# An encoder layer on one core: operand buffers of three stages moved, queries transposed without doubled rows, a division moved to VectorE

## The chip, the core and the metric

The kernel runs on one core of a Trainium2 chip. A core has TensorE (matrix products; the profile calls its products PE and its weight loads PEld), VectorE (DVE), ScalarE (ACT), GpSimd (POOL) and SyncE (SP), which here only issues DMAs. Each engine takes its instructions in the order in which they were laid down and stops at one whose operand is not ready. The metric is the device time of one execution in microseconds, the median of several runs. The profile is of one further execution.

## The reference

Two sequences of 512 rows and 1024 columns go through one encoder layer. All of it is float32.

```python
h = rms_norm(x, ln1)
q, k, v, u, g_att, g_ssm = jnp.split(h @ w_in, IN_SPLITS, axis=-1)
q = rms_norm(q.reshape(bsz, seq_len, N_HEADS, HEAD_DIM), q_gain)
k = rms_norm(k.reshape(bsz, seq_len, N_KV_HEADS, HEAD_DIM), k_gain)
y_att = windowed_attention(q, k, v, sink, bias, band_mask(seq_len))
y_ssm = s5_branch(u, ...)        # bidirectional linear recurrence, GELU, gate
mixed = sigmoid(g_att) * y_att + sigmoid(g_ssm) * y_ssm
x = x + mixed @ w_out
h2 = rms_norm(x, ln2)
y = x + jnp.square(jax.nn.relu(h2 @ w_up)) @ w_down
```

The attention has 16 query heads of 64 columns, four to each of 4 key heads. A block of 128 queries sees its own block of keys and its two neighbours, with a relative bias and a sink logit for each head. The MLP is 1024 to 4096 to 1024.

## The kernel before, in words

**Numbers in two parts.** TensorE works on a rounded format (fp32r). To keep float32's precision, every operand is split: `hi` is the value rounded by ScalarE, `lo` the rest, subtracted by VectorE. A product is three matmuls, hi·hi, hi·lo and lo·hi (`mm3`, L148 to L152). Nearly all matmuls have 128 weight columns and a moving operand of 512 (in the projections of queries 256) columns.

**Memory.** SBUF is laid out as two stacks of pools. On the left stand the constants, among them `vec`, a tile of 66 columns (L108), and above it `cpool` (tiles c_hi, c_lo and c_raw, weights split for the column products), `evp` and the pools of each stage. On the right stands first `hT`, the normalised input turned and split, later four slots of 32 KB, `slot_a` to `slot_d`. Sizes of the tiles below a tile fix its address. Worked out from them, before the change the tiles of `cpool`, `evp` and the T4 operand of the up projection start at 352 modulo 512 bytes, and the tiles on the right at 480.

**Stages in order of time** (us of the profile):

- to 233: x is normalised and turned into `hT`, then the tables of the recurrence are built. All through this and the next two stages, column products of `hT` with w_in (L221, a generator called by `pull`) are fed to TensorE as a filler between the stage's own matmuls.
- 233 to 342: the scan, 62 steps of VectorE operations (from L582), each depending on the one before, with filler on TensorE.
- 342 to 481: output of the recurrence, key products (L261), first projections of queries and values.
- 481 to 718: attention, in 8 steps (key head j, sequence sq), numbered 0 to 7.
- 718 to 835: last division of the attention, then the gate (GLU) with products of `act` and c_hi, c_lo.
- 835 to 937: output projection and second norm.
- 937 to 1241: up projection. Sixteen tiles r, for each seven products of one step of a Strassen scheme (a product of 2 by 2 blocks in seven block products; the operands are B11 and B21 in `slot_c`, T1 and B22 in `slot_d`, T2 and T3 in `slot_b`, T4 on the left). The raw weights of the tiles are split into a ring of operands in `slot_a`. Results are rounded through ReLU and square (`relu2`, ScalarE, L1182 and L1183) and stored to `a_scr`.
- 1248 to 1562: down projection, `product_d`, again seven products, each over the 16 tiles taken in pairs.

**The attention's order.** TensorE, ScalarE and VectorE run in the order of the code inside `tc.manual_schedule`; SyncE's and GpSimd's instructions are placed by the planner. Each step has four units (qb 0 to 3, a block of 128 queries each). A unit computes the scores of four heads (`scores`, L764), row maxima (`largest`, VectorE, L768), exponentials (`exp`, ScalarE, L774), and beside them, for the unit before, the transposes of P (`turn`, L780), their split (`high` ScalarE L784, `low` VectorE L789) and the products with V (`value`, L796). `add` (VectorE, L806) joins the two halves of the unit before into `ya`. As fill between them stands `Tile` for the next step: `project` (L711), `square`, `power` (GpSimd, L724), `norm` (VectorE, L728), then the doubling copy on GpSimd (L729), which writes every query's 64 values a second time, so that the transpose (`turn`, L734) gives 128 rows: values in rows 0 to 63 and again in rows 64 to 127. `high` (ScalarE, L739) writes the scaled and rounded values into all 128 rows and `low` (VectorE, L743) then puts the rest into the lower 64, so one matmul of 128 rows multiplies the high and the low part at once with keys that stand in both halves.

**The division.** The softmax is divided at the end. In step i, unit 1, `Divide` takes the row sums of step i−1: `invert` (VectorE), `turn` (a transpose of 16 columns on TensorE, L822, a copy, a DMA of the inverses to `rs_scr`, L825, and two DMAs from there that spread a row over 64 partitions, `fac`, L830). At the end of that unit `multiply` is laid down: GpSimd multiplies `ya` (128 by 1024) by `fac` (L835), and the queue of SyncE stores the result. The last step's division stands alone after the loop, with GpSimd's queue, and the gate's loads of `mx` (L1036) follow it.

**The down projection's buffers.** A pair needs `d_a` (activations from `a_scr`, 4 KB a partition, three buffers), a tile `k1_r` of weights (k1, k2 and k3 stay for later products, 4 KB each), and the split tiles a_hi, a_lo, b_hi, b_lo. Before, the pool `down0` (k1_0 to k1_2, d_a, a_hi) lies in the place of the ring, `down` (a_lo, b_hi, b_lo, xq) in that of `slot_b`, and `downb` (k1_3 to k1_7) in that of `slot_c`. The ring is read until the last product of the last tile, p4; `slot_c` is read last by p2 of that tile.

Of the kernel before, what the change touches and what calls it, by code (L numbers as in the profile page):

```python
# [12 lines left out]
F32 = mybir.dt.float32  # L13
F32R = mybir.dt.float32r
I32 = mybir.dt.int32
AF = mybir.ActivationFunctionType
ALU = mybir.AluOpType
AX = mybir.AxisListType

P = 128  # L20
# [6 lines left out]
HALF = 512  # L27
# [3 lines left out]
G = 4  # L31
HD = 64
# [8 lines left out]
CH = 16  # L41
# [22 lines left out]
def hybrid_layer(ctx, tc, x, rel, onehot, ln1, w_qkv, w_ug, vectors, lam, coefs, w_glu, w_out, ln2,  # L64
                 w_up, w_down, out):
    nc = tc.nc
    V, S, PE, GP, SP = nc.vector, nc.scalar, nc.tensor, nc.gpsimd, nc.sync
    DRAM, PSUM = bass.MemoryType.DRAM, bass.MemoryType.PSUM

    const = ctx.enter_context(tc.tile_pool(name="const", bufs=1))  # L70
# [33 lines left out]
    ident = const.tile([P, P], F32, name="ident")  # L104
    make_identity(nc, ident)
    neg_half = const.tile([P, 16], F32, name="neg_half")
    V.memset(neg_half, -0.5)
    vec_pad = const.tile([P, 66], F32, name="vec")  # L108
    vec = vec_pad[:, 0:58]
    bglu_sb, gain_q, gain_k, nsink = [vec[:, a:b] for a, b in ((0, 8), (8, 9), (9, 10), (10, 26))]  # L110
    dd = vec[:, 26:58].rearrange("p (x g) -> p x g", g=2)
# [58 lines left out]
    cf = coef_cm.__enter__()  # L170
# [9 lines left out]
    fi = cf.tile([P, GROUPS], F32, name="fi")  # L180
    es = cf.tile([P, 9, GROUPS], F32, name="es")
    bs_p = cf.tile([P, GROUPS, T], F32, name="bs_p")
    dmask = cf.tile([P, CH], F32, name="dmask")
    lbt = cf.tile([P, 2, SB, 64], F32, name="lbt")
    columns = [("u", U_BLK + c) for c in range(KT)] + [("a", GA_BLK + c) for c in range(KT)] + [("s", GS_BLK + c) for c in range(KT)]
    loaded, key_tiles, sigmoids = [], [], set()
# [446 lines left out]


    with tc.tile_pool(name="att", bufs=2, reuse_waits="tile") as ap, tc.tile_pool(name="attc", bufs=1, reuse_waits="tile") as ac:
        kn = ac.tile([P, NT, N_KV, HD], F32, name="kn")
        va = ac.tile([P, NT, N_KV, P], F32R, name="va")

# [59 lines left out]
        class Tile:  # L698
# [25 lines left out]
                GP.tensor_tensor(self.rq, ms, neg_half[:, 0:G], op=ALU.pow)  # L724

            def norm(self):
                self.qn = ap.tile([P, G, 2, HD], F32, tag="qn", name="qn")
                V.tensor_mul(self.qn[:, :, 0], self.psv, self.rq[:, :, None].to_broadcast([P, G, HD]))  # L728
                GP.tensor_copy(self.qn[:, :, 1], self.qn[:, :, 0])  # L729

            def turn(self):
                self.pt = acc()
                for h in range(G):
                    PE.transpose(self.pt[:, h * P:(h + 1) * P], self.qn[:, h].rearrange("p a d -> p (a d)"), ident)  # L734

            def high(self):
                self.ptv = self.pt.rearrange("p (h t) -> p h t", h=G)
                self.dst = queries[self.key][:, :, self.t * P:(self.t + 1) * P]
                S.activation(self.dst, self.ptv, AF.Copy, scale=gain_q)  # L739

            def low(self):
                dst = self.dst[64:128]
                V.scalar_tensor_tensor(dst, self.ptv[64:128], gain_q[64:128], dst.bitcast(F32),  # L743
                                       op0=ALU.mult, op1=ALU.subtract)

        class Unit:
# [61 lines left out]
        class Divide:  # L808
# [23 lines left out]

            def multiply(self):
                j, sq = self.j, self.sq
                GP.tensor_tensor(self.ya, self.ya, self.fac, op=ALU.mult)  # L835
                self.queue.dma_start(mix_scr[2 * j:2 * j + 2, :, sq * HALF:(sq + 1) * HALF].rearrange("m p t -> p m t"),
                                     self.ya)

# [52 lines left out]
        with tc.manual_schedule(engines={mybir.EngineType.PE, mybir.EngineType.Activation, mybir.EngineType.DVE}):  # L891
            for i, (j, sq) in enumerate(steps):
                nxt = steps[i + 1] if i + 1 < len(steps) else None
                sums = small.tile([P, G, NB], F32, tag="sm", name="sm", bufs=2)
                ya = ap.tile([P, 2, HALF], F32, tag="ya", name="ya")
                extra = pieces_of(i)
                for qb in range(NB):
                    if 1 <= i < 3:

                        t = (i - 1) * NB + qb  # L900
                        SP.dma_start(y2_scr[:, :, t, :].rearrange("g c k -> c g k"), y_scr[t])
                    cur = Unit(j, sq, qb, sums, ya)
                    n3 = prev.nkb if prev else 0
                    div = Divide(*steps[i - 1], *done) if qb == 1 and i > 0 else None
                    new = Tile(*nxt, qb) if nxt else None
                    project = new.project if new else nop
                    kd = None
                    if rows and not rows.qn:
                        rows.power()
                    cur.scores(0)  # L910
                    cur.largest(0)
                    cur.scores(1)
                    if owed:
                        owed.add()
                    cur.largest(1)
                    if n3:
                        prev.turn(0)
                        prev.high(0)
                    project(6)
                    if n3:  # L920
                        prev.low(0)
                    cur.exp(0)
                    cur.exp(1)
                    if rows and not rows.qn:
                        rows.norm()
                    if qb == 0 and nxt:
                        kd = key_copies(*nxt)
                    if div:
                        div.invert()
                    cur.scores(2)  # L930
                    cur.largest(2)
                    if n3:
                        prev.turn(1)
                        prev.high(1)
                    project(4)
                    if n3:
                        prev.value(0, 0)
                    project(2)
                    cur.exp(2)
                    cur.scores(3)  # L940
                    if lower:
                        lower()
                        lower = None
                    if n3:
                        prev.low(1)
                        prev.value(0, 1)
                    cur.largest(3)
                    if rows:
                        rows.turn()
                    if n3 > 2:  # L950
                        prev.turn(2)
                    if kd:
                        key_turn(*nxt, kd)
                    if div:
                        div.turn()
                    project(4)
                    if rows:
                        rows.high()
                        rows.low()
                    if n3 > 2:  # L960
                        prev.high(2)
                    if n3:
                        prev.value(1, 0)
                    cur.exp(3)
                    if n3 > 2:
                        prev.low(2)
                    project(4)
                    if n3:
                        prev.value(1, 1)
                    project(4)  # L970
                    if n3 > 2:
                        prev.value(2, 0)
                        prev.value(2, 1)
                    if new:
                        new.square()
                    if n3:
                        prev.lower_part()
                    if extra:
                        lower = extra.pop(0)()
                    if div:  # L980
                        div.multiply()
                    owed, prev, rows = prev, cur, new
                    if nxt and qb == NB - 1 and sq == 1:
                        load_biases(nxt[0])
                done = sums, ya
                if i == len(steps) - 2:
                    hpool_cm.__exit__(None, None, None)
                    slot_a = opers.enter_context(tc.tile_pool(name="slot_a", bufs=1, side="right", reuse_waits="tile"))
                    slot_b = opers.enter_context(tc.tile_pool(name="slot_b", bufs=1, side="right", reuse_waits="tile"))
                    yT = [slot(slot_b), slot(slot_a)]  # L990
# [9 lines left out]
        div = Divide(*steps[-1], *done, True)  # L1000
# [231 lines left out]
    opers.close()  # L1232


    with tc.tile_pool(name="down0", bufs=2, side="right", reuse_waits="tile") as d0, \
            tc.tile_pool(name="down", bufs=2, side="right", reuse_waits="tile") as dp, \
            tc.tile_pool(name="downb", bufs=1, side="right", reuse_waits="tile") as db, \
            tc.tile_pool(name="downc", bufs=1, reuse_waits="tile") as dc:

        k1 = [(d0 if r < 3 else db).tile([P, 2, HALF], F32, name=f"k1_{r}", bufs=1) for r in range(NPAIR // 2)]  # L1240
        k2, k3 = [[dc.tile([P, 2, HALF], F32, name=f"k{i}_{r}") for r in range(NPAIR // 2)] for i in (2, 3)]
        q1, q3, q4, q5 = [dc.tile([P, 4, HALF], F32, name=f"q{i}") for i in (1, 3, 4, 5)]

        def product_d(n):

# [149 lines left out]
```

## Time and profile before

| what | value |
|---|---|
| median of 3 runs | 1566.19 us (1565.89 to 1566.23) |
| the profiled execution, time | 1564.48 us |
| its span | 1562.7 us |
| mean granted TensorE clock | 0.986 |
| ScalarE busy | 771.0 us (49%) |
| GpSimd busy | 231.0 us (15%) |
| DMA | 237.07 MB, 152 GB/s on the mean |

The page of the profile gives busy time by engine, the chain of work that ended last, and the costliest groups: `line engine op out<-in partitions x elements xcount | busy, mean ns of one | idle time of the engine before them and what ended it`. `L1263 ACT CAST a_hi<-d_a ... x56 | 59.0, 1054` is line 1263 on ScalarE, 56 times, 59.0 us in all, 1054 ns each. In a timeline, each row is a start, a duration, an engine, a line and an operation, and in brackets how long the engine sat idle before it and what it waited for. A row of the view by windows gives the stretch, its length, busy time and count for TensorE, its weight loads, VectorE, ScalarE and GpSimd, then the granted TensorE clock, the mean busy share of the DMA engines and GB/s. Matmuls overlap in their records, so their rate is read from start to start, not from a duration. PEq, ACTq and SPq are the sequencers of the engines, which issue DMAs.

### The profile page before, as it was taken

Reading aid. Unit: us, or ns where it says so; the run is one execution under the profiler, and the core shown is the slowest. Engines: PE = TensorE matmul, PEld = TensorE weight load, DVE = VectorE, ACT = ScalarE, POOL = GpSimd, SP = SyncE. Lnnn points to the kernel's source line nnn. Section 1 sums busy time; section 2 is a strip of 40 time slices with the busy share of each in tenths; the row PEclk is TensorE's granted clock in tenths of the full one; section 3 lists DMA queues with packets and bytes.
Section 4 is the critical chain, followed back from the end, with each engine's and each line's share of the span. In section 5 each row is a group of like instructions: output and inputs, shape, how many; then the busy total and the mean of one; then the engine's idle time right before and its main releaser. Section 6 shows DMA issues by size and latency. Waiting matters only on the chain.

```text
span 1562.7 us, 21589 instructions
## 1 busy us (share of the span) xinstructions
PE 1480.6 (95%) x7818; PEld 1242.0 (79%) x7818; DVE 1104.4 (71%) x1989; ACT 771.0 (49%) x1349; POOL 231.0 (15%) x412
## 2 busy tenths in 40 slices
PE   5899999999999999988799989999999899999998
PEld 4688888878999888975577867888888687888787
DVE  8688849985436888896875558777777478566553
ACT  6577761224436788785333335544455334433332
POOL 3133332002331333323320000000000000000000
PEclk9899999999999999999899999999999999999999
DMA  5644438227751323125745234444443694455332
GB/s 180 213 156 158 146 137 301 101 88 268 266 169 40 104 56 101 62 77 174 228 148 170 81 108 138 155 155 159 157 153 122 228 340 145 148 161 163 121 122 68
DMA packets 103532, 237.07 MB, mean 152 GB/s; under 512 B 11994, under 2 KB 31706, under 8 KB 103424
## 3 DMA queue, kind: packets, MB, share of 16 engines
q1 hardware_dynamic: 64784, 134.82, 27.0%
q0 software_dynamic: 16464, 50.39, 9.8%
q10 hardware_dynamic: 22176, 50.47, 8.4%
q8 instruction: 62, 1.02, 0.3%
q14 instruction: 46, 0.38, 0.1%
HBM read 165.35 MB, written 81.82 MB: 158 GB/s over the span
## 4 chain that ended last, share of the span: by engine, by line
PE 40%; issue 7%; DMA 2%; DVE 2%; POOL 2%; ACT 1%; POOLq 0%; ACTq 0%; DVEq 0%; SPq 0%
PE bank L151 13%; PE bank L152 13%; PE bank L150 13%; POOL mx L1036 1%; DMA w_raw<-in_w_out_dram 0%; DMA mx<-ga_scr 0%; DMA k<-in_w_down_dram 0%; DMA fac<-rs_scr 0%; DVE rn_xn L1116 0%; DMA f_raw<-in_w_up_dram 0%; ACT rn_xn L1112 0%; PE acc L152 0%; POOL rs L1115 0%; DMA mx<-mix_scr 0%; PE acc L151 0%
## 5 line engine op out<-in xcount | busy, mean ns | idle before, releaser
L221 PE MATMUL acc<-hT,c_hi 128*128 128x512 f32 x768 | 252.5, 404 | 0.7 <-ACT c_hi L211 0.7
L150 PE MATMUL bank<-b_hi,a_hi 128*128 128x512 f32 x448 | 174.0, 391 | 7.2 <-ACT b_hi L1263 7.2
L151 PE MATMUL bank<-b_lo,a_hi 128*128 128x512 f32 x448 | 175.4, 392 | 2.5 <-DVE b_lo L1264 2.5
L152 PE MATMUL bank<-b_hi,a_lo 128*128 128x512 f32 x448 | 174.8, 390 | 0.0
L221 PEld LDWEIGHTS acc<-hT,c_hi 128*128 128x128 f32 x768 | 142.5, 190 | 32.2 <-issue 2.2
L221 PE MATMUL acc<-hT,c_lo 128*128 128x512 f32 x384 | 154.7, 403 | 0.5 <-DVE c_lo L212 0.5
L150 PE MATMUL bank<-act,act 128*128 128x512 f32 x376 | 147.2, 392 | 3.0 <-ACT act L1161 3.0
L1263 ACT CAST a_hi<-d_a 128x1024 fp32r<-128x1024 f32 x56 | 59.0, 1054 | 183.4 <-PE bank L151 181.0
L151 PE MATMUL bank<-act,act 128*128 128x512 f32 x376 | 146.9, 391 | 0.0
L152 PE MATMUL bank<-act,act 128*128 128x512 f32 x376 | 146.4, 390 | 0.0
L1264 DVE TENSOR_TENSOR a_lo<-d_a,a_hi 128x1024 fp32r<-128x1024 f32 x56 | 68.5, 1224 | 107.4 <-ACT a_hi L1263 107.4
L711 PE MATMUL acc<-w_hi,hT 128*128 128x256 f32 x512 | 115.4, 294 | 0.0
L150 PEld LDWEIGHTS bank<-b_hi,a_hi 128*128 128x128 f32 x448 | 84.4, 189 | 25.3 <-ACT b_hi L1263 7.7
L151 PEld LDWEIGHTS bank<-b_lo,a_hi 128*128 128x128 f32 x448 | 84.5, 189 | 21.5 <-DVE b_lo L1264 4.1
L152 PEld LDWEIGHTS bank<-b_hi,a_lo 128*128 128x128 f32 x448 | 84.5, 189 | 17.6
L711 PEld LDWEIGHTS acc<-w_hi,hT 128*128 128x128 f32 x512 | 86.4, 188 | 3.6
L221 PEld LDWEIGHTS acc<-hT,c_lo 128*128 128x128 f32 x384 | 72.9, 190 | 16.3 <-issue 1.0
L150 PEld LDWEIGHTS bank<-act,act 128*128 128x128 f32 x376 | 71.0, 189 | 18.4 <-ACT act L1161 3.4
L151 PEld LDWEIGHTS bank<-act,act 128*128 128x128 f32 x376 | 71.0, 189 | 14.8
L152 PEld LDWEIGHTS bank<-act,act 128*128 128x128 f32 x376 | 70.8, 188 | 14.8
L774 ACT ACTIVATE p<-p,nmx 128x257 f32<-128x257 f32 (+1 forms) x128 | 72.2, 565 | 15.9 <-DVE nmx L768 14.9
L1182 ACT ACTIVATE a<-a 128x512 f32<-128x512 f32 x64 | 40.5, 633 | 73.5 <-DVE a L1176 50.3
(316 smaller groups left out, 3536.7 us busy)
## 6 DMA issues: line engine op xcount, KB each, us to landing
d_a<-a_scr SPq DMA_DIRECT2D x56, 512.0 KB, 3.6
u_raw<-in_w_up_dram SPq DMA_DIRECT2D x32, 512.0 KB, 5.6
a_scr<-t ACTq DMA_DIRECT2D x64, 256.0 KB, 5.0
k<-in_w_down_dram SPq DMA_DIRECT2D x32, 512.0 KB, 5.9
c_raw<-in_w_ug_dram SPq DMA_DIRECT2D x48, 256.0 KB, 3.2
a_scr<-a ACTq DMA_DIRECT2D x48, 256.0 KB, 2.2
ct_scr<-ctab POOLq DMA_DIRECT2D x16, 576.0 KB, 4.4
ctab_in<-ct_scr POOLq DMA_DIRECT2D x16, 576.0 KB, 7.2
```

What stands on the lines that cost most here:

```text
L150: PE.matmul(ps, a[0], b[0], start=first, stop=False)
L151: PE.matmul(ps, a[0], b[1], start=False, stop=False)
L152: PE.matmul(ps, a[1], b[0], start=False, stop=last)
L221: PE.matmul(ps, w[wi][:, k, :], hT[s][hi][:, k, :], start=n == 0, stop=n == 3 * KT - 1)
L711: PE.matmul(self.ps, hT[sq][act][:, k, col:col + P], w[:, k % 4, :], start=i == 0, stop=i == 3 * KT - 1)
L774: S.activation(p, p, AF.Exp, bias=self.nmx[:, h:h + 1], scale=-1.0, accum_out=self.sums[:, h, self.qb:self.qb + 1])
L1036: GP.dma_start(t_, scr[m, :, s * HALF:(s + 1) * HALF])
L1182: S.activation(c, c, AF.Relu)
L1263: S.copy(hi, src)
L1264: V.tensor_sub(lo, src, hi.bitcast(F32))
```

## The change

Four things change.

1. **Addresses.** The tile `vec` grows from 66 to 98 columns (128 bytes), and a mask of 16 columns, before in a pool on the right, moves into it. All that stands above it on the left moves up by 128 bytes, `cpool`, `evp` and T4's operand from 352 to 480 modulo 512. In the attention's pool an unused tile of 40 columns is put first, so that its tiles move by 288 bytes in all.
2. **Queries.** `norm` writes 64 values for a query and the copy on GpSimd is gone. The transpose has 64 weight columns and gives 64 rows; `high` writes rows 0 to 63, and `low` reads them there and writes rows 64 to 127.
3. **Division.** `multiply` is VectorE's and stands in unit 3 of the step, behind the first row maximum, no longer at the end of unit 1. The last one is VectorE's too.
4. **Down projection.** `downb` comes first (in the ring's place), filled up with q5 and an unused tile of 4 KB; `down0` comes third (in the place of `slot_c`); `down` stays in that of `slot_b`.

```diff
-    vec_pad = const.tile([P, 66], F32, name="vec")
+    vec_pad = const.tile([P, 98], F32, name="vec")
...
-    dmask = cf.tile([P, CH], F32, name="dmask")
+    dmask = vec_pad[:, 64:64 + CH]
...
+        ap.tile([P, 40], F32, name="apart", bufs=1)
...
-                self.qn = ap.tile([P, G, 2, HD], F32, tag="qn", name="qn")
-                V.tensor_mul(self.qn[:, :, 0], self.psv, self.rq[:, :, None].to_broadcast([P, G, HD]))
-                GP.tensor_copy(self.qn[:, :, 1], self.qn[:, :, 0])
+                self.qn = ap.tile([P, G, HD], F32, tag="qn", name="qn")
+                V.tensor_mul(self.qn, self.psv, self.rq[:, :, None].to_broadcast([P, G, HD]))
...
-                    PE.transpose(self.pt[:, h * P:(h + 1) * P], self.qn[:, h].rearrange("p a d -> p (a d)"), ident)
+                    PE.transpose(self.pt[0:64, h * P:(h + 1) * P], self.qn[:, h], ident)
...
-                S.activation(self.dst, self.ptv, AF.Copy, scale=gain_q)
+                S.activation(self.dst[0:64], self.ptv, AF.Copy, scale=gain_q[0:64])
...
-                V.scalar_tensor_tensor(dst, self.ptv[64:128], gain_q[64:128], dst.bitcast(F32),
+                V.scalar_tensor_tensor(self.dst[64:128], self.ptv, gain_q[0:64], self.dst[0:64].bitcast(F32),
                                        op0=ALU.mult, op1=ALU.subtract)
...
-                GP.tensor_tensor(self.ya, self.ya, self.fac, op=ALU.mult)
+                V.tensor_mul(self.ya, self.ya, self.fac)
...
                     cur.largest(0)
+                    if qb == 3 and late:
+                        late.multiply()
                     cur.scores(1)
...
-                    if div:
-                        div.multiply()
+                    if qb == 1:
+                        late = div
...
-    with tc.tile_pool(name="down0", bufs=2, side="right", reuse_waits="tile") as d0, \
+    with tc.tile_pool(name="downb", bufs=1, side="right", reuse_waits="tile") as db, \
             tc.tile_pool(name="down", bufs=2, side="right", reuse_waits="tile") as dp, \
-            tc.tile_pool(name="downb", bufs=1, side="right", reuse_waits="tile") as db, \
+            tc.tile_pool(name="down0", bufs=2, side="right", reuse_waits="tile") as d0, \
...
+        q5 = db.tile([P, 4, HALF], F32, name="q5")
+        db.tile([P, HALF * 2], F32, name="apart")
...
-        q1, q3, q4, q5 = [dc.tile([P, 4, HALF], F32, name=f"q{i}") for i in (1, 3, 4, 5)]
+        q1, q3, q4 = [dc.tile([P, 4, HALF], F32, name=f"q{i}") for i in (1, 3, 4)]
```

More of the change, by code (lines that the diff above doesn't have):

```diff
@@ L733, in turn @@
                 for h in range(G):
-                    PE.transpose(self.pt[:, h * P:(h + 1) * P], self.qn[:, h].rearrange("p a d -> p (a d)"), ident)
+                    PE.transpose(self.pt[0:64, h * P:(h + 1) * P], self.qn[:, h], ident)
             def high(self):
-                self.ptv = self.pt.rearrange("p (h t) -> p h t", h=G)
+                self.ptv = self.pt[0:64].rearrange("p (h t) -> p h t", h=G)
                 self.dst = queries[self.key][:, :, self.t * P:(self.t + 1) * P]
-                S.activation(self.dst, self.ptv, AF.Copy, scale=gain_q)
+                S.activation(self.dst[0:64], self.ptv, AF.Copy, scale=gain_q[0:64])
             def low(self):
-                dst = self.dst[64:128]
-                V.scalar_tensor_tensor(dst, self.ptv[64:128], gain_q[64:128], dst.bitcast(F32),
+                V.scalar_tensor_tensor(self.dst[64:128], self.ptv, gain_q[0:64], self.dst[0:64].bitcast(F32),
                                        op0=ALU.mult, op1=ALU.subtract)
```

## The prediction

> **What bounds the kernel now.** I read the page first (engine totals, chain of work, costliest groups), then TensorE's waits, then the places that they name.
>
> ```profile
> span 1562.7 us, 21589 instructions
> PE 1480.6 (95%) x7818; PEld 1242.0 (79%) x7818; DVE 1104.4 (71%) x1989; ACT 771.0 (49%) x1349; POOL 231.0 (15%) x412
> PE 40%; issue 7%; DMA 2%; DVE 2%; POOL 2%; ACT 1%; POOLq 0%; ACTq 0%; DVEq 0%; SPq 0%
> ...
> L221 PE MATMUL acc<-hT,c_hi 128*128 128x512 f32 x768 | 252.5, 404 | 0.7 <-ACT c_hi L211 0.7
> L221 PE MATMUL acc<-hT,c_lo 128*128 128x512 f32 x384 | 154.7, 403 | 0.5 <-DVE c_lo L212 0.5
> ```
>
> TensorE is busy for 95% of the span and leads the chain. So the time moves in three ways only: TensorE waits less, its matmuls follow each other faster, or it is made to wait anew. Its list of waits has the two that the change aims at:
>
> ```profile
> PE bank L150 <- ACT b_hi L1263: 7.2, 1, 7.2
> ...
> PE acc L734 <- POOL qn L729: 6.0, 16, 2.2
> ```
>
> The sum is made against the profiled execution, 1564.48 us with a span of 1562.7; the median of the three runs is 1566.19, 1.7 more. I take the difference that I work out off that median.
>
> **A. From up to down projection.** In the timelines of SyncE, ScalarE and TensorE and the table by windows:
>
> ```profile
> 1227.62 2.42 SPq L1253 DMA_DIRECT2D k<-in_w_down_dram  x5
> 1232.83 0.38 SPq L1274 DMA_DIRECT2D xq<-x_scr  x1
> 1241.06 0.33 SPq L1250 DMA_DIRECT2D d_a<-a_scr  x1
> ...
> 1243.46 0.63 ACT L1183 ACTIVATE a<-a 128x512 f32<-128x512 f32 x1 [0.34 <-ACT a L1182]
> 1245.25 1.04 ACT L1263 CAST a_hi<-d_a 128x1024 fp32r<-128x1024 f32 x1 [1.16 <-DMA d_a<-a_scr]
> 1247.39 1.04 ACT L1263 CAST b_hi<-k 128x1024 fp32r<-128x1024 f32 x1 [1.10 <-DMA k<-in_w_down_dram]
> ...
> 1240.87 0.40 PE L152 MATMUL bank<-t,act 128*128 128x512 f32 x1
> 1248.49 1.22 PE L150 MATMUL bank<-b_hi,a_hi 128*128 128x512 f32 x2 [7.22 <-ACT b_hi L1263]
> ...
> 1248.40:1252.50 4.10, 3.98 (x9) 2.67 (x10) 2.45 (x2) 2.09 (x3) 0.00 (x0) 0.50 1.04 415
> ```
>
> The three issue times are those at which the three slots come free: the first sequence's slot at 1227.62, the next at 1232.83, the ring at 1241.06, with the last up product. Now the first operands (d_a, k1_0 to k1_2) lie in the ring and the weights k1_3 to k1_7, not needed yet, in the slot that is free first. The change swaps them. The first operands are then issued from 1227.6; by the page's medians they land 3.6 us (d_a) and 5.9 us (k) later, so before 1236, and the casts (1.04 each on ScalarE, 1.22 the subtraction on VectorE) can end before 1241. The stall is the distance from 1241.10 (one spacing after 1240.87) to 1248.49, 7.4 us. Behind it the granted clock is 0.50 and nine matmuls take 3.98 us; at 0.227 each they would take 2.04, so 1.9 more goes. Together −9.3 at most. The five late weights now wait for the ring (1241) and are first needed three pairs into the product: a pair is 24 matmuls of 0.227, 5.4 us, so at 1257; they are hidden, with about 10 us of room. At the other end stands ScalarE's queue: if the casts come behind the last squares (1243.46 and 0.63), two casts more give 1246.2, which saves 2.3 of the wait and perhaps some of the slow clock. I take **−9.0** (−2.3 to −9.3); ScalarE's idle time before 1245.25 is waiting for the DMA, which speaks for the near end. q5 changes its place only and costs nothing.
>
> **B. Operands moved in address.** The longer vector tile shifts the left side by 128 bytes: c_hi, c_lo, the T4 operand t and others go from residue 352 to 480 of 512, where hT, the slots and the down buffers already lie (worked out from the tile sizes). Nothing else differs between these two stretches of one stream of up products:
>
> ```profile
> 1218.50 0.39 PE L150 MATMUL bank<-act,act 128*128 128x512 f32 x1
> 1218.73 0.39 PE L151 MATMUL bank<-act,act 128*128 128x512 f32 x1
> ...
> 1219.18 0.40 PE L150 MATMUL bank<-t,act 128*128 128x512 f32 x1
> 1219.88 0.39 PE L150 MATMUL bank<-t,act 128*128 128x512 f32 x1
> ...
> 260.00:330.00 70.00, 70.00 (x303) 56.76 (x302) 67.68 (x176) 14.72 (x25) 0.00 (x0) 1.00 0.34 122
> 1330.00:1430.00 100.00, 100.00 (x443) 82.78 (x442) 66.68 (x64) 38.76 (x41) 0.00 (x0) 1.00 0.53 168
> ```
>
> Both operands at 480: 0.227 from start to start, and 100/443 = 0.226 over a long stretch. One at 352: 0.70 for three, 0.233, and 70/303 = 0.231 in the scan stage (L221). So a matmul of 512 columns may gain 5.5 ns. How many are on the path? Of the 1152 on L221, 416 lie in the table stage (16 steps of 26 by the code; I take TensorE as its bound): −2.3. Some 481 fill the scan, where VectorE's chain sets the end (below): nothing. Of the other 255 I count 150: −0.8. Products of act with c_hi and c_lo in the gate stage (by the code 8 columns, 2 sequences, 24 each, 384): I take 300 as off the waits, −1.7. T4, 16 tiles of 12: 192 × 6 = −1.2. Query projections in attention (by the code 768 of 256 columns): 2.6 ns each for the half of them whose weights come to 480, −1.0. Sum −7.0.
>
> ```profile
> L582 DVE TENSOR_TENSOR t<-h,a8r x62: 417/424/427, 233.2 to 339.9; 128x256 f32<-128x256 f32 x62
> ...
> 347.46 0.71 PE L615 MATMUL sps<-st,ctab_in 128*128 128x128 f32 x4 [1.40 <-ACT st L595]
> ```
>
> The scan is 62 dependent steps on VectorE. TensorE's filler is already 1.40 us early at its end; 481 × 5.5 ns = 2.6 make that wait 4.0, and so it may lose clock as at 1248: +0.9 as an estimate (0 to 1.7, under the 1.9 seen after 7.2 us). B is **−6.1** (0 to −13; the far end has all 2,900 such matmuls gain 4.5 ns on average).
>
> The Trainium skill speaks against this: "TensorE: Matmul & The Clock Gate", Part 2, step ①, has two independent read ports, so that loading the next weights takes no bandwidth from the running matmul; by it the addresses would change nothing and B would be 0. The rows above have 0.227 beside 0.233 and do not agree, unless something else in t is the cause.
>
> **C. Attention.** Each of the eight steps (0 to 7) has four units. Below stand the fourth of step 1, the first and the fourth of step 2, and the first two of step 4 (a step without disturbance):
>
> ```profile
> 530.10:537.06 6.96, 6.96 (x56) 6.59 (x54) 5.70 (x16) 5.29 (x14) 1.85 (x4) 1.00 1.04 283
> 537.06:545.92 8.86, 6.65 (x54) 6.21 (x52) 5.31 (x16) 5.12 (x14) 4.68 (x6) 1.00 0.25 87
> 561.30:568.94 7.64, 7.14 (x55) 6.58 (x54) 5.81 (x16) 5.30 (x14) 3.79 (x5) 1.00 0.18 69
> 597.78:604.29 6.51, 6.51 (x53) 6.19 (x52) 5.31 (x16) 5.12 (x14) 2.34 (x5) 1.00 0.02 4
> 604.29:611.40 7.11, 6.89 (x52) 6.30 (x51) 6.91 (x18) 6.07 (x16) 1.85 (x4) 1.00 0.08 27
> ...
> L835 POOL TENSOR_TENSOR ya<-ya,fac 128x1024 f32<-128x1024 f32 x7 | 16.7, 2392 | 15.6 <-DMA fac<-rs_scr 15.6
> L729 POOL COPY qn<-qn 128x256 f32<-128x256 f32 x28 | 11.1, 397 | 27.6 <-DVE qn L728 27.5
> ...
> L1264 DVE TENSOR_TENSOR a_lo<-d_a,a_hi 128x1024 fp32r<-128x1024 f32 x56 | 68.5, 1224 | 107.4 <-ACT a_hi L1263 107.4
> ```
>
> Removed: 28 copies of 0.40 on GpSimd between the norm and the transpose. TensorE waited 6.0 for them, 2.2 of it in one place, where the division's 2.4 us stood ahead of the copy (unit 537.06: 8.86 against 6.51 of its like). That unit falls back, −2.3, and the fourth one of that step (7.64 against 6.96) −0.7. Of the other 3.8 half returns as VectorE's wait (the second unit has it busy 6.91 of 7.11): −1.9. Added: the multiplication on VectorE. No such operation stands there now; the same size elsewhere takes 1.22 (L1264), GpSimd's took 2.39, and I take 1.22 as the same engine's. The fourth unit leaves it 6.96 − 5.70 = 1.26, so it just fits, but it stands ahead of the sum, the subtraction of P and the norm: +0.15 in each of six steps (0 to 1.2). Regular part: −3.0 − 1.9 + 0.9 = −4.0.
>
> Transposes of 64 weight columns in place of 128 (128 of them by the code):
>
> ```profile
> 608.91 0.66 PE L734 MATMUL acc<-ident,qn 128*128 128x128 f32 x4 [0.22 <-POOL qn L729]
> 609.40 0.27 PE L822 MATMUL tps<-ident,rsum 128*16 128x128 f32 x1
> 609.43 0.37 PE L711 MATMUL acc<-w_hi,hT 128*128 128x256 f32 x1
> ```
>
> Five transposes take 0.52 us, 0.10 each, the one with 16 columns among them, so I take 0 (0 to −6.5, half of 128 × 0.10). The Trainium skill has a load's time go with its column count (the same page, section LDWEIGHTS); by it the far end would hold. The copies to 64 partitions keep their row length and cost what they did.
>
> The new **wait**: the multiplication comes behind largest(0) of unit 4, about 1.0 us into it, and VectorE takes its instructions in order.
>
> ```profile
> 527.13 0.33 SPq L668 DMA_DIRECT2D w_raw<-in_w_qkv_dram  x1
> 528.12 1.28 SPq L830 DMA_DIRECT2D fac<-rs_scr  x2
> ...
> DMA to landing us min/median/max: 6.4/6.7/7.1
> ...
> 560.85 2.39 POOL L835 TENSOR_TENSOR ya<-ya,fac 128x1024 f32<-128x1024 f32 x1 [1.79 <-DMA fac<-rs_scr]
> ```
>
> In step 1 the two loads of fac go out at 528.12 and some 0.64 later, behind a weight load, and the second lands 7.1 later, at 535.8. VectorE gets there at 530.10 + 1.0 = 531.1. It stands 4.7 us; behind it on VectorE are the sum over halves, P's low part, the row maxima and the norm; TensorE waits for all of them, the first value product at once. +4.9 with the refill, and +1.5 for the clock (estimate under the 1.9 above): +6.4. In step 2 fac lands at 560.85, before its unit 4 begins (561.30); I expect no wait there, and none in the later steps, where the loads go out as in step 2. C is **+2.4** (−4.0 without the wait).
>
> **D. The last division**, alone on its path, takes 1.22 on VectorE for 2.4: −1.2; step 7, without a next projection, pays most of its own multiplication, +0.9: **−0.3** (−1.2 to +1.2).
>
> **Sum:** −9.0 − 6.1 + 2.4 − 0.3 = −13.0: 1551.5 as profiled, **1553.2** as median.
>
> **Rivals.**
> 1. No wait in step 1, because the loads of fac go out ahead of the weight load: −19.4, 1546.8. For it: a planner may order SyncE anew. Against: the row 527.13. Chance 0.23.
> 2. The address does nothing (as the page named under B would have it): −6.9, 1559.3. For: a port of its own for weights would do so; against: 0.227 beside 0.233. 0.09.
> 3. Narrow transposes halve (the rule of section LDWEIGHTS): −6.5 more, 1546.7. Against: the 16-column row. 0.05.
> 4. The casts of the down stage stand behind the last squares: A is −3.5, 1558.7. 0.09.
> 5. Slower: SyncE puts the loads of fac behind a blocked load in every step, as in step 1, since a piece of the next heads' weights may be due there. Each such wait costs 6.4 in unit 4; the gain without any is 19.4, so from the fourth on the kernel is slower: four give 25.6 − 19.4 = +6.2, 1572.4. Against: the row at 560.85. 0.06.
>
> The forecast keeps 0.48. The range, 1543 to 1560.5, takes in cases 1 to 4; below case 1 it leaves some 4 for the far end of B or the narrow transposes, above case 2 a little over 1. About 0.2% (3.1 us) is what a measurement of this kernel can tell from no change; faster by more 0.89, within 0.05, slower 0.06.
>
> **What would show it.** A: d_a issued near 1227 less the shift, no wait of bank on b_hi, clock 1.00 throughout. B: spacing of L221 and of t,act 0.227; the wait on st longer. C: no row for L729; a VectorE multiplication of 1.22, in step 1 idle some 4.7 us for fac; the first unit of step 2 at 6.5. D: mx starts 1.2 us sooner behind the last fac. Wrong would be: spacing unchanged, the stall at b_hi still over 3 us, or VectorE waiting for fac in more steps than one.

## The result and the profile after

The changed kernel takes 1556.06 us (median of 4 runs, 1555.1 to 1560.3) against 1566.21 for the kernel before (4 runs): a ratio of 0.994, 95% interval 0.9921 to 0.9959, so −10.1 us. Forecast were −13.0 and 1553.2, with a range of 1543 to 1560.5. The profiled execution took 1555.4.

The first lines of its page, which answer to those shown of before:

```profile
span 1553.6 us, 21555 instructions
PE 1474.7 (95%) x7818; PEld 1246.7 (80%) x7818; DVE 1110.6 (71%) x1997; ACT 768.1 (49%) x1349; POOL 200.6 (13%) x372
...
L221 PE MATMUL acc<-hT,c_hi 128*128 128x512 f32 x768 | 249.9, 401 | 0.8 <-ACT c_hi L211 0.8
L221 PE MATMUL acc<-hT,c_lo 128*128 128x512 f32 x384 | 153.3, 400 | 0.5 <-DVE c_lo L212 0.5
```

TensorE still leads. Its list of waits has lost the two at which the change aimed, b_hi with 7.2 us and qn with 6.0, and has two that are new or larger:

```profile
PE po L795 <- DVE ya L805: 5.3, 2, 4.5
PE po L795 <- DVE pl L788: 4.8, 9, 1.0
...
PE acc L150 <- ACT gl L1048: 3.3, 2, 1.8
```

To see where the 9.1 us between the two profiled executions came from, one compares the same instruction's start in both. The first score of the attention comes 2.8 earlier than before (478.1 for 480.9). The last product with V comes 3.6 later (721.1 for 717.5), so the attention alone lost 6.3. The first down matmul comes 5.3 earlier (1243.1 for 1248.5), although the last up matmul comes 2.1 later (1242.9 for 1240.9), and the last down matmul 9.1 earlier; from the first to the last down matmul it is 306.1 for 309.8. The change gains at both ends and loses in the middle.

**From up to down.** Timelines of SyncE, ScalarE and TensorE and one row of the windows, after:

```profile
1229.77 0.33 SPq L1253 DMA_DIRECT2D d_a<-a_scr  x1
1230.20 0.38 SPq L1256 DMA_DIRECT2D k<-in_w_down_dram  x1
...
1233.43 1.05 ACT L1266 CAST a_hi<-d_a 128x1024 fp32r<-128x1024 f32 x1 [1.61 <-DMA d_a<-a_scr]
1235.18 1.06 ACT L1266 CAST b_hi<-k 128x1024 fp32r<-128x1024 f32 x1 [0.70 <-PE bank L152]
...
1242.92 0.39 PE L152 MATMUL bank<-t,act 128*128 128x512 f32 x1
1243.14 0.39 PE L150 MATMUL bank<-b_hi,a_hi 128*128 128x512 f32 x1
...
1243.00:1247.10 4.10, 4.10 (x20) 3.40 (x19) 2.65 (x5) 1.81 (x3) 0.00 (x0) 1.00 1.03 380
```

The loads of the first operands are issued 13 us before they are needed, and the first two casts end 7 us before. The first down matmul follows the last up matmul after 0.22, as any other, and 20 matmuls fit into 4.1 us where there were nine, at a clock of 1.00.

**The wait in the attention.** Timelines of SyncE, VectorE and TensorE, SyncE's wait between 510 and 530, and the windows of step 1's fourth unit and of three stretches of it, after:

```profile
517.54 0.36 SPq L669 DMA_DIRECT2D w_raw<-in_w_qkv_dram  x1
523.48 0.33 SPq L669 DMA_DIRECT2D w_raw<-in_w_qkv_dram  x1
523.86 0.52 SPq L900 DMA_DIRECT2D y_scr<-y_scr  x1
524.47 1.28 SPq L829 DMA_DIRECT2D fac<-rs_scr  x2
...
SPq L669 <- DVE w_lo L671: 5.5, 1, 5.5
...
531.76 1.23 DVE L834 TENSOR_TENSOR ya<-ya,fac 128x1024 f32<-128x1024 f32 x1 [4.38 <-DMA fac<-rs_scr]
...
533.89 0.77 PE L795 MATMUL po<-ph,va 128*128 128x512 f32 x1 [4.51 <-DVE ya L805]
...
526.45:539.64 13.19, 8.68 (x55) 7.90 (x54) 6.73 (x16) 5.37 (x14) 1.46 (x3) 0.87 0.79 221
533.89:534.50 0.61, 0.61 (x2) 0.51 (x3) 0.61 (x3) 0.20 (x1) 0.00 (x0) 0.50 0.95 359
536.00:537.00 1.00, 1.00 (x6) 0.93 (x5) 0.60 (x3) 0.41 (x3) 0.00 (x0) 0.50 0.68 186
537.50:538.50 1.00, 1.00 (x10) 0.95 (x9) 0.93 (x2) 0.96 (x4) 0.19 (x1) 1.00 0.36 68
```

Read from the top: SyncE issues one weight load at 517.54 (0.36 us) and then stands 5.5 for VectorE's `w_lo`, which is made from the buffer that the next weight load fills. That load goes out at 523.48, and only behind it the loads of fac. VectorE stands 4.38 for fac, TensorE 4.51 for the sum behind the multiplication. When TensorE goes on, its granted clock is 0.50 up to 537.0, and 1.00 from 537.5 on. The unit takes 13.19 where it took 6.96.

### The profile page after: what moved, and what is told of

It reads as the page before. It is cut to its first block, busy times and chain, and to the rows that moved or that the text cites. A ratio compares the mean times of both kernels' runs of the same rounds, so it can differ in the third digit from the quotient of the medians.

```text
span 1553.6 us, 21555 instructions
## 1 busy us (share of the span) xinstructions
PE 1474.7 (95%) x7818; PEld 1246.7 (80%) x7818; DVE 1110.6 (71%) x1997; ACT 768.1 (49%) x1349; POOL 200.6 (13%) x372
## 4 chain that ended last, share of the span: by engine, by line
PE 53%; issue 17%; DVE 6%; DMA 3%; ACT 3%; POOL 3%; POOLq 0%; SPq 0%; DVEq 0%; ACTq 0%
PE bank L151 13%; PE bank L152 13%; PE bank L150 13%; PE acc L712 3%; PE po L795 2%; PE acc L261 1%; PE sps L763 1%; POOL mx L1037 1%; DVE pl L788 1%; PE tps L779 1%; PE sps L615 1%; DVE p L767 1%; PE acc L150 1%; PE acc L151 1%; PE acc L152 1%
## 5 line engine op out<-in xcount | busy, mean ns | idle before, releaser
L221 PE MATMUL acc<-hT,c_hi 128*128 128x512 f32 x768 | 249.9, 401 | 0.8 <-ACT c_hi L211 0.8
L221 PEld LDWEIGHTS acc<-hT,c_hi 128*128 128x128 f32 x768 | 142.5, 190 | 29.9 <-issue 2.2
L221 PE MATMUL acc<-hT,c_lo 128*128 128x512 f32 x384 | 153.3, 400 | 0.5 <-DVE c_lo L212 0.5
L221 PEld LDWEIGHTS acc<-hT,c_lo 128*128 128x128 f32 x384 | 72.9, 190 | 15.2 <-issue 1.0
L767 DVE CUSTOM_DVE_ANT_0 p<-sps,bias,vec 128x256 f32<-128x256 f32 (+1 forms) x128 | 69.1, 541 | 6.8 <-PE sps L763 5.6
```

Source lines behind the costliest of these rows:

```text
L221: PE.matmul(ps, w[wi][:, k, :], hT[s][hi][:, k, :], start=n == 0, stop=n == 3 * KT - 1)
L767: V.tensor_tensor_reduce(self.p[:, h, 1:1 + self.nk], self.s[h][:, 0:self.nk], biases[self.j][h][:, b0:b0 + self.nk], -1.0, nsink[:, hh:hh ...
```

## The experiments

All ratios are to the kernel before, on the same chip as the run.

### Each part alone

`p_down` has the order of the down pools, and q5, alone:

```diff
-    with tc.tile_pool(name="down0", ...) as d0, ... "down" ... as dp, ... "downb" ... as db, \
+    with tc.tile_pool(name="downb", ...) as db, ... "down" ... as dp, ... "down0" ... as d0, \
+        q5 = db.tile([P, 4, HALF], F32, name="q5")
+        db.tile([P, HALF * 2], F32, name="apart")
...
```

> The kernel before with the order of the down projection's pools alone. Theory (the stall of 7.4 us and the half clock behind it go): -9.3 to -11 us, 1555 to 1557, first down matmul within 0.5 us of the last up matmul, clock 1.00 there. Rival (the casts stand behind the last squares of the up projection): -2.3 to -4.2 us, 1562 to 1564.

`p_addr` has the longer `vec`, the mask in it and the unused tile in the attention's pool alone:

```diff
-    vec_pad = const.tile([P, 66], F32, name="vec")
+    vec_pad = const.tile([P, 98], F32, name="vec")
...
-    dmask = cf.tile([P, CH], F32, name="dmask")
+    dmask = vec_pad[:, 64:64 + CH]
...
+        ap.tile([P, 40], F32, name="apart", bufs=1)
```

> The kernel before with the addresses alone (vec longer, mask moved, unused tile in the attention's pool). Theory (a matmul of 512 columns takes 0.227 in place of 0.232 where both operands stand at 480 of 512): L221, act,c_hi and t,act spaced 0.227; -4 to -6 us in time, of it 2.5 to 3 up to the end of the recurrence, 1 in the up projection, nothing in the attention. Rival (ports independent of addresses): spacing 0.232 and 0 us.

`p_query` has the queries without doubled rows alone:

```diff
-                GP.tensor_copy(self.qn[:, :, 1], self.qn[:, :, 0])
...
-                    PE.transpose(self.pt[:, h * P:(h + 1) * P], self.qn[:, h].rearrange("p a d -> p (a d)"), ident)
+                    PE.transpose(self.pt[0:64, h * P:(h + 1) * P], self.qn[:, h], ident)
...
```

> The kernel before with the queries turned without doubled rows alone; the division stays on GpSimd. Theory (the copy's 0.40 goes from the way norm to transpose, transposes keep 0.109 each): first unit of step 2 at 6.5 in place of 8.86, second units 0.3 to 0.5 shorter, -5 to -6 us. Rival (transposes of 64 weight columns take half): spacing of the transposes near 0.055 and some 6 us more, -11 to -12. Rival (nothing but step 2 gains): -2.4.

`p_mul` has the multiplication on VectorE, in unit 3, alone:

```diff
-                GP.tensor_tensor(self.ya, self.ya, self.fac, op=ALU.mult)
+                V.tensor_mul(self.ya, self.ya, self.fac)
...
+                    if qb == 3 and late:
+                        late.multiply()
...
-                    if div:
-                        div.multiply()
+                    if qb == 1:
+                        late = div
```

> The kernel before with the division's multiplication on VectorE in unit 3 alone. Theory (VectorE stands for fac in step 1, and 1.22 us more in each fourth unit): +6.2 in step 1, +0.8 in each of the other fourth units, -2.4 in the first unit of step 2, -1.2 at the last division: +6 to +8 us, 1572 to 1574. Rival (the multiplication fits VectorE's idle time of the unit, only step 1 pays): +2 to +3.

| kernel | median us | ratio | 95% interval | difference us |
|---|---|---|---|---|
| p_down | 1555.92 | 0.994 | 0.992 to 0.9961 | −10.1 |
| p_addr | 1560.25 | 0.9967 | 0.9955 to 0.9979 | −5.7 |
| p_query | 1560.64 | 0.9962 | 0.9949 to 0.9976 | −5.4 |
| p_mul | 1577.23 | 1.0073 | 1.0048 to 1.0098 | +11.2 |

(Differences to 1565.99, the median of before in this set.) They add up to −10.0, and the change measured −10.1. That is a sum over the whole kernel, and each interval reaches 2 to 4 us to either side; unit by unit the parts do touch each other, as the first unit of step 2 shows below. Three parts gain 21.2 together, and the multiplication gives back 11.2, above what any of the cases named for it expected. Its windows say how:

```profile
529.40:543.34 13.94, 8.91 (x55) 8.03 (x54) 6.91 (x17) 5.37 (x14) 1.85 (x4) 0.88 0.75 210
595.23:603.31 8.08, 7.64 (x56) 6.71 (x55) 6.82 (x17) 5.29 (x14) 1.85 (x4) 1.00 0.57 163
```

Step 1 pays 7.0 (13.94 against 6.96), the fourth units of steps 3 to 5 pay 1.1 each (8.08 against 6.95) and that of step 6 1.75. That of step 2 takes 8.08 too, where before it took 7.64. The first unit of step 2 gives back 2.3 and step 7 pays another 1.4.

In `p_query` the transposes got at most a little faster. Four of them, now of 64 weight columns, take 0.44 from the first to what follows; and the weight loads (PEld) that belong to them, before, then in `p_query`:

```profile
605.48 0.60 PE L733 MATMUL acc<-ident,qn 128*64 128x128 f32 x4
605.92 0.27 PE L820 MATMUL tps<-ident,rsum 128*16 128x128 f32 x1
...
L734 PEld LDWEIGHTS acc<-ident,qn 128*128 128x128 f32 x128 | 13.7, 141 | 13.6 <-POOL qn L729 12.9
L733 PEld LDWEIGHTS acc<-ident,qn 128*64 128x64 f32 x128 | 13.8, 110 | 3.2
```

That is 0.11 each. The four at the same place before took 0.49 (608.91 to 609.40), a wait for the copy among it; in `p_addr`, which still has 128 columns, most groups without such a wait take 0.43 to 0.49. So the columns are worth at most 0.05 for four, under 2 us for all 128 (an estimate), and perhaps nothing. The Trainium skill ("TensorE: Matmul & The Clock Gate", section LDWEIGHTS) has a load's time go with its columns. The records of the loads get shorter, 110 ns on the mean for 141, but not by half, and the spacing of the transposes hardly follows. What `p_query` does gain in its profile is 0.45 in the second units of most steps (3.0 in all) and 0.9 over the third units. The first unit of step 2 did not come to 6.5 as expected but to 8.12, 0.7 less than before: the copy of keys (`kd`, L684) stands behind the same multiplication on GpSimd, and the key's transpose waits for it as the query's had.

### Where and by which engine the division is done

`a_i1end` lays step 1's multiplication at the end of its unit, `a_end` lays all of them there, `a_gp` puts all but the last on GpSimd again, at the end of unit 1. The edit of `a_end` (that of `a_i1end` has the condition on step 1 beside it):

```diff
-                    if qb == 3 and late:
-                        late.multiply()
...
                     if qb == 1:
                         late = div
+                    if qb == 3 and late:
+                        late.multiply()
```

> The changed kernel with the multiplication of step 1 alone laid down at the end of its fourth unit. Theory (the wait for fac costs 6.2 in step 1, the place 0.84 in every other step): fourth unit of step 1 at 7.0 in place of 13.2, the other fourth units stay at 7.8, so about -6 us, 1550. Rival (VectorE waits at the later place too, since fac lands later than that): -2 to -4.

> The changed kernel with the multiplication at the end of the fourth unit in all steps. Theory (in the middle of the unit it delays row maxima, P's low part and the norm, at its end it falls into VectorE's idle time of the next step's first unit): fourth units at 6.9, first units at 6.5, -6 for step 1 and -4 to -5 for the others, 1545 to 1547. Rival (VectorE has no room there either): first units 0.8 longer, no better than with step 1 alone, 1550.

> The changed kernel with all divisions but the last on GpSimd again, laid down at the end of unit 1. Theory (with the copy gone nothing of TensorE hangs on GpSimd behind the multiplication but the norm's power): fourth units at 6.9, a loss of at most 0.7 in step 2's fourth unit, -10 to -11, 1545 to 1546. Rival (the 2.4 us on GpSimd stand ahead of the power in some units): first unit of step 2 near 8.1 as with the queries alone, 1547 to 1548.

| kernel | median us | ratio | 95% interval | to the change (1556.06), us |
|---|---|---|---|---|
| a_i1end | 1549.45 | 0.989 | 0.9867 to 0.9914 | −6.6 |
| a_end | 1547.94 | 0.9884 | 0.9859 to 0.9909 | −8.1 |
| a_gp | 1545.23 | 0.9866 | 0.9847 to 0.9886 | −10.8 |

In `a_i1end` step 1's fourth unit fell from 13.19 to 6.97 and nothing else in steps 0 to 6 moved, so 6.2 was the price of the wait; step 7 took 37.4 for 35.9, and the cause of that stays open. In `a_end` the fourth units fell from 7.8 to 6.95 too, with the first units unchanged to 0.05, and step 7 fell to 33.8, its length before the change. In its profile the attention, from the first to the last product with V, takes 8.6 us less than in that of `a_i1end` (229.7 and 238.3), but the medians differ by only 1.5, inside their spread (`a_end` ran from 1543.08 to 1550.45; its profile is of the fastest execution, that of `a_i1end` of the slowest, 1553.63). How much of that gain reaches the end is therefore not settled. In `a_gp` all fourth units are at 6.95 and the one loss is the expected rival's, in the first unit of step 2 (8.12):

```profile
534.96 2.37 POOL L834 TENSOR_TENSOR ya<-ya,fac 128x1024 f32<-128x1024 f32 x1
537.28 0.60 POOL L685 COPY kd<-kn 128x512 f32<-128x512 f32 x1
...
537.93 0.66 PE L694 MATMUL tps<-ident,kd 128*128 128x128 f32 x4 [1.40 <-POOL kd L685]
```

### What makes fac late

`a_facq` has GpSimd issue the row's store and the loads of fac:

```diff
-                self.queue.dma_start(rs_scr[sq, j * G:(j + 1) * G, :]...
+                GP.dma_start(rs_scr[sq, j * G:(j + 1) * G, :]...
-                    self.queue.dma_start(self.fac[e * 64:(e + 1) * 64],
+                    GP.dma_start(self.fac[e * 64:(e + 1) * 64],
```

> The changed kernel with the row's store and the loads of fac of every division issued by GpSimd instead of SyncE. Theory (in step 1 the loads stand 6.3 us behind two weight loads on SyncE): VectorE waits under 1 us for fac, fourth unit of step 1 at 7.8 in place of 13.2, -5 to -6 us, 1550 to 1551. Rival (fac is late because its transfer is slow, the DMA engines being full there): the wait stays over 3 us, 1554 to 1556. Rival (GpSimd stops for the landed row and holds up the norm's power): the second or third units 1 to 3 us longer, no gain.

1557.23 us, ratio 0.9943 (0.9927 to 0.9959): no gain over the change. The theory holds for step 1, and the last rival for the rest. Timelines of VectorE, GpSimd and TensorE in `a_facq`:

```profile
526.23 1.22 DVE L834 TENSOR_TENSOR ya<-ya,fac 128x1024 f32<-128x1024 f32 x1
...
551.28 1.24 POOL L829 DMA_DIRECT2D fac<-rs_scr  x2 [3.50 <-DMA rs_scr<-row]
552.53 1.05 POOL L725 TENSOR_TENSOR rq<-ms,neg_half 128x4 f32<-128x4 f32 x1
...
554.10 1.06 PE L734 MATMUL acc<-ident,qn 128*64 128x128 f32 x4 [3.44 <-DVE qn L729]
```

In step 1 VectorE multiplies without any wait (the unit takes 7.79), so the place on SyncE was enough to make fac late. What held that place up was not the issue of the two weight loads, as the expectation has it (0.36 and 0.33), but the 5.5 us for which SyncE stood for `w_lo` between them. The transfer had a share in the length of the wait: the loads landed up to 6.5 after their issue in the changed kernel and up to 4.4 after it here. With 4.4 it would have landed near 529.5, 2.1 after VectorE came to it at 527.4 (an estimate from these rows), so about half of the 4.38 goes to the slower transfer. But GpSimd now stands 3.50 for the landed row in step 2, the power for the norm stands behind it, and TensorE waits 3.44: that unit takes 12.59 in place of 8.18, and the third units of steps 1, 3 and 4 take 0.7 to 0.9 longer. The stall has only changed its engine.

### The division split between two engines

`a_mix` has the division of step 1 on VectorE at the end of unit 3 (the fourth, "unit 4" in the expectation), the others on GpSimd at the end of unit 1, the last on VectorE:

```diff
-                V.tensor_mul(self.ya, self.ya, self.fac)
+                (V if self.last or (j, sq) == steps[0] else GP).tensor_tensor(self.ya, self.ya, self.fac, op=ALU.mult)
...
+                    if qb == (3 if i == 1 else 1) and late:
+                        late.multiply()
```

> The changed kernel with the divisions on GpSimd at the end of unit 1, but that of step 1 on VectorE at the end of unit 4 and the last one on VectorE. Theory (the one collision left on GpSimd, first unit of step 2 at 8.1, goes; nothing else changes): first unit of step 2 at 6.5, 1.6 less than with GpSimd in all steps, 1543 to 1544. Rival (the gate stage gives it back): 1545.

1542.5 us (5 runs, 1542.28 to 1544.6), ratio 0.9849 (0.9835 to 0.9863): −23.4 to the 1565.86 of before in its set. Step 2's first unit, by the windows:

```profile
531.24:537.75 6.51, 6.51 (x53) 6.24 (x52) 5.96 (x17) 5.17 (x14) 2.01 (x4) 1.00 0.36 126
```

TensorE is busy for all of it. This is clearly faster than the change. The 2.7 under `a_gp` is more than the 1.6 forecast, but the intervals of the two overlap, so which of these two is faster is not shown.

### Which addresses

`a_pad64` is the changed kernel with `vec` at 82 columns, the left side at 416 modulo 512.

```diff
-    vec_pad = const.tile([P, 98], F32, name="vec")
+    vec_pad = const.tile([P, 82], F32, name="vec")
```

> The changed kernel with the vector tile 64 bytes shorter, so that the left side stands at 416 of 512. Theory (the product is fast only with both operands at 480 of 512): L221 and t,act spaced 0.232 to 0.233 again. Rival (any place but 352 does, or one that is alike modulo 64): 0.227.

A single run, 1559.11 us. Rows of the timeline of TensorE and of the windows, first `a_pad64`, then the changed kernel:

```profile
1224.95 0.39 PE L150 MATMUL bank<-t,act 128*128 128x512 f32 x1
1225.65 0.39 PE L150 MATMUL bank<-t,act 128*128 128x512 f32 x1
...
260.00:330.00 70.00, 70.00 (x307) 57.44 (x306) 67.67 (x175) 15.78 (x27) 0.00 (x0) 1.00 0.36 128
```

```profile
1221.38 0.39 PE L150 MATMUL bank<-t,act 128*128 128x512 f32 x1
1222.06 0.39 PE L150 MATMUL bank<-t,act 128*128 128x512 f32 x1
...
260.00:330.00 70.00, 70.00 (x310) 58.03 (x309) 67.67 (x175) 15.79 (x27) 0.00 (x0) 1.00 0.37 130
```

With t, the moving operand, at 416, three matmuls take 0.70 as before the change (0.233 each); at 480 they take 0.68 (0.227). For L221, whose weights moved and whose moving operand did not, 70 us hold 303 before, 307 at 416 and 310 at 480. Nothing but addresses differs here, so it is not something else in t that made it slow. The theory holds for t and only in part for weights.

## Why the prediction was right, and where it was not

**A, right.** −9.0 forecast, −10.1 measured alone. The wait and the slow clock both went. The forecast's far end, −9.3, was close; the excess of 0.8 lies within the interval of the measurement. The profiles give a place where more could come from: from the first to the last down matmul it is 309.8 before, 306.7 in `p_down` and 306.1 in the changed kernel, 3 to 4 less where the prediction counted 1.9. `a_gp` and `a_mix`, with the same pools, have 308.3 and 308.6, so this size is not settled.

**B, the sum right in part by luck, three of its terms wrong.** −6.1 forecast, −5.7 measured. The mechanism held: 0.227 where both operands stand at 480. The Trainium skill's rule on independent read ports ("TensorE: Matmul & The Clock Gate", Part 2, step ①) gave 0 for this, and the measurement differs from it. But the scan was to give nothing, with a longer wait at its end (+0.9), and gave about 3. From the first scan step to the first product with the states it is 114.3 us before (233.2 to 347.46), 114.2 and 114.7 in `p_mul` and `p_query`, 112.4 in `a_pad64`, and 111.2 in both `p_addr` and the changed kernel. That product came 2.7 earlier in the changed kernel, while the last scan step stood where it was (339.89 and 340.02). The step that failed is "VectorE's chain sets the end". Timelines of ScalarE, before, then after:

```profile
345.88 0.59 ACT L236 COPY sg<-acc 128x512 f32<-128x512 f32 x1 [3.37 <-PE acc L221]
346.36 2.03 ACT L595 COPY st<-h 64x512 f32<-64x512 f32 x2
```

```profile
343.14 0.59 ACT L236 COPY sg<-acc 128x512 f32<-128x512 f32 x1 [3.24 <-PE acc L221]
343.63 2.03 ACT L595 COPY st<-h 64x512 f32<-64x512 f32 x2
```

The copy of the states, which TensorE waits for, stands on ScalarE behind the copy of the last filler product, and that waits for TensorE. The wait of 1.40 was put down to ScalarE, and its cause was TensorE's own backlog; so faster filler did move it. The attention's term (−1.0) was not there: in `p_addr` the units are as long as before. And the gate stage kept none of its −1.7. TensorE's waits between 800 and 830 and the windows of this stretch, before, then after:

```profile
812.19 0.50 PE L152 MATMUL acc<-act,c_lo 128*128 128x512 f32 x1 [0.96 <-DVE c_lo L122]
800.00:830.00 30.00, 28.79 (x123) 22.41 (x122) 20.41 (x32) 11.52 (x19) 3.76 (x7) 1.00 0.41 136
```

```profile
812.65 0.50 PE L150 MATMUL acc<-act,c_hi 128*128 128x512 f32 x1 [1.50 <-ACT gl L1048]
814.09 0.80 PE L152 MATMUL acc<-act,c_lo 128*128 128x512 f32 x1 [0.71 <-DVE c_lo L122]
800.00:830.00 30.00, 27.79 (x116) 22.33 (x115) 19.74 (x32) 11.41 (x20) 4.30 (x8) 0.94 0.46 143
```

The products are faster, run up to the gate's values and weights, and wait 1.25 longer. Behind these waits the clock falls as well, to 0.94 on the mean of the stretch, which it did not do before; 116 matmuls fit into it for 123. `p_addr` shows the same clock of 0.94. So the terms of the attention and the gate (2.7 together) were not there, and the scan, put at nothing, took their place. What the table stage and T4 gave by themselves was not measured apart.

**C, mechanism right, one term mis-sized.** The wait in step 1 was forecast at +6.4 and measured at 6.2 (13.19 against 6.96), for the reason given, and with a clock of 0.50 behind it. The removal of the copies was forecast at about −4.9, and `p_query` measured −5.4, but its parts were others: the 2.3 in the first unit of step 2 go when the division leaves GpSimd (`p_mul` alone has them), without the copy alone only 0.7 go, and the second and third units gave 3.9, where 1.9 was forecast for all but step 2. The step that failed is "it just fits" of the multiplication: +0.15 in each fourth unit was forecast. Windows of the fourth and the first unit of step 4, and two rows of VectorE, after:

```profile
619.19:626.97 7.78, 7.65 (x55) 6.72 (x54) 6.67 (x17) 5.28 (x14) 1.46 (x3) 1.00 0.42 137
597.87:604.35 6.48, 6.48 (x53) 6.23 (x52) 5.38 (x16) 5.04 (x13) 2.00 (x4) 1.00 0.02 4
...
620.03 1.22 DVE L834 TENSOR_TENSOR ya<-ya,fac 128x1024 f32<-128x1024 f32 x1
621.17 0.84 DVE L805 TENSOR_TENSOR ya<-po,ol 64x256 f32<-64x256 f32 x2
```

VectorE is busy for 6.67 of 7.78, so the same work has room in 6.95. But 1.22 in one piece, ahead of the sum, pushes every later result of the unit, and TensorE stops at P's low part in between (the row pl L788, 9 times, 4.8 in all). That is +0.8 in steps 3 to 5 and +1.7 in step 6. In step 2 it is 7.79 for 7.64, where a fall to 6.96 was forecast; `p_addr`, with neither part of the change, has 6.96 there. `a_end` has the same work at the unit's end at no cost to the unit, so it was the place and not the amount. C and D together were forecast at +2.1 and came to +5.8 (the sum of `p_mul` and `p_query`); this 3.7 is more than the 2.9 by which the whole forecast missed, A and B together giving 0.7 back.

**D, one term right, one too small.** From the last multiplication to the loads of `mx` it took 2.3 (732.44 to 734.74) for 3.5 (728.86 to 732.34), −1.2 as forecast. Step 7 was to pay +0.9 and paid 2.1 in the changed kernel (35.9 us from its first score to the last product with V, for 33.8) and 1.4 in `p_mul`; with the multiplication at the unit's end (`a_end`) it pays nothing. So D came out nearer +0.9 than −0.3, at the upper part of its own range.

**The rivals.** The address that does nothing, the narrow transposes that halve and the casts behind the squares fell. The one of a wait in every step fell too: within the steps VectorE stands for fac in step 1 alone (4.38; its only other wait for fac, 4.05, is at the last division). The kernel without the wait did not come by itself, but `a_i1end` built it: 1549.45, against 1546.8 forecast; the fourth units, still at 7.8, can account for the difference.

## What to carry to other kernels

An operation moved to an engine with idle time costs nothing only where that idle time lies; on an engine that works in order, look at what is queued behind it and who waits for that, and put it where the queue runs dry. A wait for a DMA should stand on the engine and at the place that has least behind it: moving it from VectorE to GpSimd moved the stall with it. When a wait is put down to an engine, look one step further, at what that engine was itself waiting for: at the scan's end it was TensorE, and on SyncE's queue it was VectorE.

## What the runs showed that was not expected

- Where an operand lies sets a matmul's rate: 303, 307 and 310 matmuls in the same 70 us of the scan, with the weights at 352, 416 and 480 modulo 512, and the stage's end follows (114.3, 112.4 and 111.2 us from the first scan step). Key products of 256 columns go the other way in the median duration of their records (283 ns at 480, 276 at 416). Which pairs of places are fast, and why, was not settled.
- The stage before the scan ends at times up to 2.4 us apart in kernels that share its code: the first scan step starts at 231.3 in `p_down` and at 233.7 in `p_query`. Single executions of two kernels can differ by that without a cause in the change.
- Behind a wait of TensorE of 4.51 us the clock was 0.50 for some 3 us. In the gate stage two waits of 1.50 and 0.71 close together were followed by a mean clock of 0.79 over 812 to 820, where one of 0.96 before the change left it at 1.00.
